# Two of the four sums of weight blocks of the gate/up units go from VectorE to GpSimd

## The chip, the core and the metric

The kernel runs on one core of a Trainium2 chip. The metric is the device time of one execution in microseconds (us). The core has five engines with queues of their own: TensorE (PE), VectorE (DVE), ScalarE (ACT), GpSimd (POOL) and SyncE (SP), which here only issues DMAs. Everything is computed in float32.

## The reference

Two layers (DEPTH = 2) of a streaming encoder run over 512 tokens of a new stream and 8 × 16 tokens of running streams, 640 tokens in all, with a model width of 1024:

```python
def _swiglu(h, w_gu, w_down):
    gu = h @ w_gu
    g, u = jnp.split(gu, 2, axis=-1)
    return (jax.nn.silu(g) * u) @ w_down
...
for l in range(DEPTH):
    xp = xp + 0.5 * _swiglu(_rmsnorm(xp, norm_ffn1[l]), w_ffn1_gu[l], w_ffn1_down[l])
    ...   # the mixer: one projection w_in, a short convolution, banded attention, gates, w_o
    xp = xp + mp
    xp = xp + 0.5 * _swiglu(_rmsnorm(xp, norm_ffn2[l]), w_ffn2_gu[l], w_ffn2_down[l])
```

The same is done for `xs`, the running streams. The feed-forward width D_FF is 2816, which is 22 tiles of 128. A final RMSNorm follows. The four feed-forward blocks are called a0, b0, a1 and b1 in the kernel; a mixer lies between a and b of each layer.

## The kernel before

All 640 tokens stay in SBUF, with the model width on the partitions (`x[0]` to `x[7]`, 128 x 640 each). Weights are streamed from HBM in chunks of 128 x 1024, in the order in which they are used, into three buffers `raw`. Each float32 factor is split into a high part (`hi`, a cast to fp32r on ScalarE) and a low part (`lo`, the rest, a subtraction on VectorE), and a product is three matmuls: hi·hi, hi·lo and lo·hi. For weights the parts are `whi` (L296) and `wlo` (L301), with three buffers each.

Most products of the feed-forward blocks are made "by seven". A product is cut into 2 x 2 blocks (two halves of the output or of the tokens, two halves of the depth), and seven block products do the work of eight, in return for sums of blocks of the weights and of the tokens. For a gate/up unit `j` (`gate_up`) the blocks are the up and the gate columns of one tile of D_FF and the even and odd tiles of the model width; for a unit of the down projection (`down_rows`, "rows" units, two for each group of four `j`, named r0 and r1) they are pairs of output rows and pairs of `j`. Both kinds take their weights as a unit of kind "gu": two chunks `ra` and `rb` from HBM, and four slabs for TensorE. `source(i)` makes the slabs. Slab 0 is `ra` as it came. For slab 1, two sums are put into a tile of their own, `s65`: `rb`'s two halves added, and that plus `ra`'s first half. For slab 2, two sums are put into `ra` in place: its first half plus `rb`'s first half, and `s65`'s first half plus its second half. Slab 3 is `rb`'s second half. The sums of slab 2 can only be made when slab 0 has been split, since they overwrite it. In the profile the four sums are `s<-raw`, `s<-s,raw`, `raw<-raw,raw` and `raw<-s,raw`, all of line L240 (`add`). There are 114 such units, 84 gate/up and 30 rows units. The mixer's units (kind "mix") have three sums of other halves ahead of one of slab 2.

In a gate/up unit TensorE does the seven products in the order X11, X21, XN6, XT5, XT7, X22, XT4, on three PSUM tiles `pa`, `pb` and `pc` from a pool of four banks. `pa` is added to four times, and copied or added out in between, so that each eviction has to end before the next product starts on it: X11's copy is `c1` (L819), XN6's is `u2` (L832), then VectorE takes `g` after XT7 (L240) and after XT4 (L848). After that ScalarE applies Silu (L849). In a rows unit `A` (`da` in the profile) is used in the same way; VectorE adds parts into `x` (`take`, L980), and others are copied out by ScalarE and added to `x` by accumulating DMAs that GpSimd issues (`send`, L975).

The order of instructions on each engine is set in two ways. In the parts between, a scheduler orders them by priority and by its own estimates of their durations; `manual_schedule` takes engines out of its hands. At a block's start and end TensorE, VectorE and ScalarE follow the program; from the third unit by seven on only TensorE does, and VectorE, ScalarE and GpSimd are placed by the scheduler. `prep`, `ahead` and `begin` set at which point of the program a slab is made.

Of the kernel before, what the change touches and what calls it, by code (L numbers as in the profile page):

```python
# [13 lines left out]
ALU = mybir.AluOpType  # L14
# [160 lines left out]
def trunk(ctx: ExitStack, tc: tile.TileContext, xin, wst, small, pbias, samplebias, kcache, vcache,  # L175
          yout, ko, vo, co):
    nc = tc.nc
    PE, DVE, ACT, POOL, SP = nc.tensor, nc.vector, nc.scalar, nc.gpsimd, nc.sync
# [40 lines left out]
    slabs, n = [], 0  # L219
# [9 lines left out]
    sums, pool, spool = {}, [None], [None]  # L229

    def load(i):
        while len(raws) <= i:
            n = len(raws)
            raw = wp.tile([P, CH], F32, tag="raw", name=f"raw{n}", bufs=3)
            raws.append(raw)
            SP.dma_start(raw, wst[n])
        return raws[i]

    def add(out, a, b):
        DVE.tensor_tensor(out=out, in0=a, in1=b, op=ALU.add)  # L240

    h1, h2 = slice(0, CH // 2), slice(CH // 2, CH)
# [3 lines left out]
    def source(i):  # L246

        if i >= len(slabs):
            return None
        if i not in sources:  # L250
            kind, n, arg = slabs[i]
            ra = load(n)
            if kind == "plain":
                sources[i] = [(ra, slice(0, arg))]
            elif arg == 0:
                sources[i] = [(ra, whole)]
            else:
                rb = load(n + 1)
                if arg == 1 and kind == "gu":
                    st = sums[n] = pool[0].tile([P, CH], F32, tag="s65", name=f"s65_{n}", bufs=1)  # L260
                    add(st[:, h2], rb[:, h1], rb[:, h2])
                    add(st[:, h1], st[:, h2], ra[:, h1])
                    sources[i] = [(st, whole)]
                elif arg == 1:

                    flush()
                    st = sums[n] = spool[0].tile([P, CH // 2], F32, tag="s6", name=f"s6_{n}", bufs=1)
                    add(ra[:, h1], ra[:, h1], rb[:, h1])
                    add(st, ra[:, h1], rb[:, h2])
                    add(rb[:, h1], rb[:, h1], rb[:, h2])  # L270
                    sources[i] = [(st, h1), (rb, h1)]
                elif arg == 2:
                    if kind == "gu":
                        add(ra[:, h1], ra[:, h1], rb[:, h1])
                    add(ra[:, h2], sums.pop(n)[:, h1], ra[:, h2])
                    sources[i] = [(ra, whole)]
                else:
                    sources[i] = [(rb, h2)]
        return sources[i]
# [3 lines left out]
    def prep(i):  # L283

        if i < len(ready) or i >= len(slabs):
            return
        assert i == len(ready)
        parts = source(i)
        hi = wp.tile([P, CH], F32R, tag="whi", name=f"whi{i}", bufs=3)
        lo = wp.tile([P, CH], F32R, tag="wlo", name=f"wlo{i}", bufs=3)  # L290
        ready.append((hi, lo))
        o = 0
        for src, c in parts:
            d = slice(o, o + c.stop - c.start)
            o = d.stop
            ACT.copy(hi[:, d], src[:, c])  # L296
            pending.append((lo[:, d], src[:, c], hi[:, d]))

    def flush():
        for lo, src, hi in pending:  # L300
            DVE.tensor_tensor(out=lo, in0=src, in1=hi.bitcast(F32), op=ALU.subtract)  # L301
        pending.clear()
# [16 lines left out]
    def ahead():  # L319

        source(len(ready))
# [157 lines left out]
    class Expand(Stats):  # L479
# [72 lines left out]
        def weights(self, m):  # L552


            if m == KT - 3:
                source(used[0] + 3)
            elif m == KT - 1:
                self.flush()
                ahead()
                flush()  # L560
                begin()
# [1327 lines left out]
```

## Time and profile before

| | |
|---|---|
| median of 3 runs | 2528.91 us (2527.09 to 2528.97) |
| profiled execution | 2527.76 us, its span 2526.0 us |
| busy: TensorE, VectorE | 2505.2 us, 2141.8 us |
| busy: ScalarE, GpSimd | 1286.6 us, 223.5 us |
| granted TensorE clock | 0.998 of full speed |

The span is from the first to the last instruction. Matmuls overlap: each one of 128 x 320 has some 0.31 us in the records, and the next one starts 0.15 us later, so a stall shows best as a start that comes later than that. VectorE's instructions overlap by some 0.08 us in the same way. A tile's last letter a or b in the profile names the block (a0 and a1, b0 and b1).

### The profile page before, as it was taken

To read this page: it belongs to the slowest core of one execution; us is meant where nothing else is said; L and a number is where in the kernel's file an instruction comes from. 1 tells how busy PE (TensorE), PEld (TensorE's weight loads), DVE (VectorE), ACT (ScalarE), POOL (GpSimd) and SP (SyncE) were. 2 spreads that over 40 slices of the span, in tenths; PEclk is the share of its full clock that TensorE was granted. 3 is DMA by queue.
4 is the path that set the end of the run, shared out by engine and by line. 5 is a ranking of instruction groups with operands and counts; after the bars stand their busy time and mean duration, and the time that the engine had idled before them with its cause. 6 is when DMAs were issued, how large, how long until landed. Compare 5 with 4: busy or idle time off the path is not lost.

```text
span 2526.0 us, 43134 instructions
## 1 busy us (share of the span) xinstructions
PE 2505.2 (99%) x17216; PEld 2443.9 (97%) x17216; DVE 2141.8 (85%) x3449; ACT 1286.6 (51%) x2038; POOL 223.5 (9%) x333
## 2 busy tenths in 40 slices
PE   8999999999999999999999999999999999999998
PEld 8999999888999999999999999998889999999998
DVE  7889999878677999998789999987786778898997
ACT  5445556665444545554455555556644445454553
POOL 0001112111000001110000111101110000011111
PEclk9999999999999999999999999999999999999999
DMA  3233445235222224443223444433342222243444
GB/s 136 76 95 104 120 118 134 107 109 166 76 83 85 76 101 115 107 108 100 84 84 96 119 115 115 106 103 124 130 137 84 76 84 77 91 108 108 117 110 104
DMA packets 99418, 264.51 MB, mean 105 GB/s; under 512 B 11056, under 2 KB 44976, under 8 KB 99216
## 3 DMA queue, kind: packets, MB, share of 16 engines
q1 hardware_dynamic: 69696, 221.80, 26.3%
q0 software_dynamic: 28800, 39.29, 8.7%
q8 instruction: 135, 2.21, 0.4%
q10 hardware_dynamic: 720, 0.65, 0.1%
q14 instruction: 67, 0.55, 0.1%
HBM read 223.75 MB, written 7.94 MB: 92 GB/s over the span
## 4 chain that ended last, share of the span: by engine, by line
PE 86%; DVE 7%; ACT 3%; DMA 2%; issue 2%; SPq 0%; ACTq 0%; DVEq 0%; POOLq 0%
PE pab L386 11%; PE paa L386 10%; PE pcb L386 6%; PE pca L386 5%; PE py L363 4%; PE daa L953 4%; PE po L363 4%; PE qa L386 4%; PE pdb L363 4%; PE dab L953 3%; PE pda L363 3%; PE pbb L386 3%; PE pba L386 2%; DVE wlo L301 2%; PE pv L1395 2%; PE ma_cv L386 2%
## 5 line engine op out<-in xcount | busy, mean ns | idle before, releaser
L296 ACT CAST whi<-raw 128x1024 fp32r<-128x1024 f32 (+1 forms) x566 | 508.1, 902 | 359.5 <-DVE raw L240 55.9
L301 DVE TENSOR_TENSOR wlo<-raw,whi 128x1024 fp32r<-128x1024 f32 (+1 forms) x566 | 583.4, 1034 | 126.2 <-ACT whi L296 121.2
L296 ACT CAST whi<-s 128x1024 fp32r<-128x1024 f32 (+1 forms) x150 | 142.2, 948 | 293.5 <-DVE s L240 156.5
L386 PE MATMUL pab<-xhib,whi 128*128 128x320 f32 x704 | 218.5, 310 | 1.0 <-DVE gb L240 0.6
L386 PE MATMUL pab<-xhib,wlo 128*128 128x320 f32 x704 | 217.2, 308 | 0.0
L386 PE MATMUL pab<-xlob,whi 128*128 128x320 f32 x704 | 217.2, 308 | 0.0
L386 PE MATMUL paa<-xhia,whi 128*128 128x320 f32 x640 | 198.1, 309 | 1.1 <-ACT c_a L766 0.5
L386 PE MATMUL paa<-xloa,whi 128*128 128x320 f32 x640 | 197.4, 308 | 0.0
L386 PE MATMUL paa<-xhia,wlo 128*128 128x320 f32 x640 | 197.4, 308 | 0.0
L301 DVE TENSOR_TENSOR wlo<-s,whi 128x1024 fp32r<-128x1024 f32 (+1 forms) x150 | 163.4, 1089 | 10.9 <-ACT whi L296 10.9
L975 POOL DMA_DIRECT2D x<-c_b x56 | 49.2, 1020 | 1084.9 <-DVE x L980 435.7
L386 PEld LDWEIGHTS pab<-xhib,whi 128*128 128x128 f32 x704 | 132.0, 188 | 2.5 <-DVE gb L240 1.2
L386 PEld LDWEIGHTS pab<-xlob,whi 128*128 128x128 f32 x704 | 132.1, 188 | 0.2
L386 PEld LDWEIGHTS pab<-xhib,wlo 128*128 128x128 f32 x704 | 132.0, 188 | 0.0
L975 POOL DMA_DIRECT2D x<-c_a x64 | 56.4, 1022 | 825.2 <-ACT whi L296 591.4
L386 PEld LDWEIGHTS paa<-xhia,whi 128*128 128x128 f32 x640 | 120.0, 188 | 1.9 <-ACT c_a L766 0.8
L240 DVE TENSOR_TENSOR s<-raw 128x512 f32<-128x512 f32 x114 | 78.2, 686 | 49.7 <-DMA raw<-in_wst 49.2
L386 PEld LDWEIGHTS paa<-xloa,whi 128*128 128x128 f32 x640 | 120.0, 188 | 0.1
L386 PEld LDWEIGHTS paa<-xhia,wlo 128*128 128x128 f32 x640 | 120.0, 188 | 0.0
L386 PE MATMUL pcb<-xhib,whi 128*128 128x320 f32 x352 | 108.6, 308 | 0.0
L386 PE MATMUL pcb<-xlob,whi 128*128 128x320 f32 x352 | 108.6, 308 | 0.0
L386 PE MATMUL pcb<-xhib,wlo 128*128 128x320 f32 x352 | 108.6, 308 | 0.0
(686 smaller groups left out, 7960.0 us busy)
## 6 DMA issues: line engine op xcount, KB each, us to landing
raw<-in_wst SPq DMA_DIRECT2D x380, 512.0 KB, 3.3
x<-c_a POOLq DMA_DIRECT2D x64, 160.0 KB, 3.7
x<-c_b POOLq DMA_DIRECT2D x56, 160.0 KB, 3.6
kc<-in_kcache SPq DMA_DIRECT2D x32, 256.0 KB, 3.8
vc<-in_vcache SPq DMA_DIRECT2D x16, 512.0 KB, 4.7
x<-u_a POOLq DMA_DIRECT2D x32, 160.0 KB, 4.2
x<-u_b POOLq DMA_DIRECT2D x28, 160.0 KB, 4.2
bias<-in_pbias POOLq DMA_DIRECT2D x16, 256.0 KB, 3.5
```

Of the source, the lines that this page charges most:

```text
L240: DVE.tensor_tensor(out=out, in0=a, in1=b, op=ALU.add)
L296: ACT.copy(hi[:, d], src[:, c])
L301: DVE.tensor_tensor(out=lo, in0=src, in1=hi.bitcast(F32), op=ALU.subtract)
L363: PE.matmul(ps[:, a, :HT], w, x[:, a * HT : (a + 1) * HT], start=first and j == 0, stop=last and j == 2)
L386: PE.matmul(ps, a, b, start=start and kp == 0 and j == 0, stop=stop and kp == NP - 1 and j == 2, skip_group_check=True)
L953: PE.matmul(ps[u], w, y, start=start and i == 0 and j == 0, stop=i == 1 and j == 2, skip_group_check=True)
L975: POOL.dma_start(x[ms[2 * u + r]][:, cols], z[:, u], accum_op=ALU.add)
L1395: PE.matmul(pv[t], xx[:, t * P : (t + 1) * P], w[:, kk * AW : (kk + 1) * AW], start=c == 0 and kk == 0 and j == 0, stop=c == KT // 2 - 1 a ...
```

## The change

The two sums of slab 2 of every "gu" unit are issued on GpSimd, as `tensor_tensor` instructions with the same operands in the same order. The two sums of slab 1 stay on VectorE, as do all sums of the mixer's units. Nothing else in the program text changes.

```diff
                 elif arg == 2:
                     if kind == "gu":
-                        add(ra[:, h1], ra[:, h1], rb[:, h1])
-                    add(ra[:, h2], sums.pop(n)[:, h1], ra[:, h2])
+                        POOL.tensor_tensor(out=ra[:, h1], in0=ra[:, h1], in1=rb[:, h1], op=ALU.add)
+                        POOL.tensor_tensor(out=ra[:, h2], in0=sums.pop(n)[:, h1], in1=ra[:, h2], op=ALU.add)
+                    else:
+                        add(ra[:, h2], sums.pop(n)[:, h1], ra[:, h2])
                     sources[i] = [(ra, whole)]
```

The two new instructions are lines L274 and L275 of the changed kernel, and all lines behind them move by two (L301 becomes L303, L980 becomes L982).

## The prediction

> **What bounds the kernel now.** I read the page first, then the table of stages, then the groups of VectorE, then the timeline of single units, and last what GpSimd does beside VectorE.
>
> ```profile
> span 2526.0 us, 43134 instructions
> PE 2505.2 (99%) x17216; PEld 2443.9 (97%) x17216; DVE 2141.8 (85%) x3449; ACT 1286.6 (51%) x2038; POOL 223.5 (9%) x333
> ```
>
> TensorE is busy for 99% of the span, and almost no idle time is there to be won. From the table of stages, a stretch inside a feed-forward block:
>
> ```profile
> core 0: us, PE busy (x) PEld busy (x) DVE busy (x) ACT busy (x) POOL busy (x), PEclk, DMA share, GB/s
> 300.00:400.00 100.00, 100.00 (x684) 100.00 (x683) 94.09 (x149) 52.23 (x77) 11.53 (x14) 1.00 0.40 110
> ```
>
> TensorE has no hole there, at full clock; VectorE is next with 94%, GpSimd is nearly free. So a change that only relieves VectorE is worth what few stalls of TensorE VectorE causes there; a change that makes a weight slab or an eviction late costs full price. The list of TensorE's waits (us in total, times, longest) gives those that VectorE causes in the units in question:
>
> ```profile
> PE pab L386 <- DVE gb L240: 0.6, 2, 0.5
> ...
> PE daa L953 <- DVE x L980: 0.6, 3, 0.2
> PE dab L953 <- DVE x L980: 0.6, 3, 0.2
> ...
> PE paa L386 <- DVE ga L240: 0.4, 1, 0.4
> ```
>
> **What is moved.** From the groups of VectorE by form:
>
> ```profile
> L240 DVE TENSOR_TENSOR raw<-s,raw 128x512 f32<-128x512 f32 x150 | 102.7, 684 | 0.0
> L240 DVE TENSOR_TENSOR raw<-raw,raw 128x512 f32<-128x512 f32 x150 | 102.3, 682 | 1.1 <-DMA raw<-in_wst 0.4
> L240 DVE TENSOR_TENSOR s<-s,raw 128x512 f32<-128x512 f32 x114 | 78.2, 686 | 1.9
> ```
>
> The third row counts the "gu" units: 114 (84 gate/up, 30 down rows). Each loses one add of the first two groups, 228 in all; the other 36 of each are the mixer's and stay. The built order of the changed program shows just that: 228 rows fewer on VectorE, 228 more on GpSimd, TensorE's and SyncE's order unchanged, 114 casts on ScalarE that now wait for GpSimd. One gate/up unit, VectorE, then ScalarE, then TensorE:
>
> ```profile
> 377.28 0.68 DVE L240 TENSOR_TENSOR s<-raw 128x512 f32<-128x512 f32 x1
> 377.88 1.22 DVE L301 TENSOR_TENSOR wlo<-raw,whi 128x1024 fp32r<-128x1024 f32 x1
> 379.02 0.48 DVE L240 TENSOR_TENSOR ga<-paa,c_a 128x320 f32<-128x320 f32 x1
> 379.42 0.68 DVE L240 TENSOR_TENSOR s<-s,raw 128x512 f32<-128x512 f32 x1
> 380.02 0.48 DVE L840 TENSOR_TENSOR ga<-ga,rhoa 128x320 f32<-128x320 f32 x1
> 380.42 0.48 DVE L240 TENSOR_TENSOR ua<-pca,c_a 128x320 f32<-128x320 f32 x1
> 380.82 0.68 DVE L240 TENSOR_TENSOR raw<-raw,raw 128x512 f32<-128x512 f32 x1
> 381.42 0.68 DVE L240 TENSOR_TENSOR raw<-s,raw 128x512 f32<-128x512 f32 x1
> 382.12 0.49 DVE L848 TENSOR_TENSOR ga<-paa,rhoa 128x320 f32<-128x320 f32 x1
> 382.52 1.22 DVE L301 TENSOR_TENSOR wlo<-s,whi 128x1024 fp32r<-128x1024 f32 x1
> ```
> ```profile
> 380.25 1.05 ACT L296 CAST whi<-s 128x1024 fp32r<-128x1024 f32 x1 [1.79 <-PE pca L386]
> 382.21 1.05 ACT L296 CAST whi<-raw 128x1024 fp32r<-128x1024 f32 x1 [0.91 <-DVE raw L240]
> 383.17 0.74 ACT L849 ACTIVATE ga<-ga 128x640 f32<-128x640 f32 x1
> 383.88 0.43 ACT L819 COPY c_a<-paa 128x320 f32<-128x320 f32 x1
> ```
> ```profile
> 383.68 0.31 PE L386 MATMUL pba<-xhia,whi 128*128 128x320 f32 x1
> 385.44 0.31 PE L386 MATMUL paa<-xhia,whi 128*128 128x320 f32 x1
> ```
>
> Removed: 382.12 − 380.82 = 1.30 us of VectorE a unit. None of it is on TensorE's path here: the second add ends at 382.10, the third slab is cast at 382.21, and TensorE goes on at 383.68 and 385.44 without a hole. A unit has seven products of 385.44 − 383.68 = 1.76 us, 12.3 us, so 8.1 units fall into 100 us and VectorE's load there drops from 94 to 83.5. That alone is worth nothing to TensorE.
>
> What waits behind the new adds: on ScalarE the cast of the third slab, behind it the Silu (L849) and the copy of the first product (L819), which frees `paa` for the matmul at 385.44. The copy ends at 384.31, so it has 1.1 us. On VectorE nothing waits for GpSimd by a semaphore but the third slab's `wlo`.
>
> **Price of an add on GpSimd.** The trace has no such add. The nearest rows are one-input copies of GpSimd, left alone and beside VectorE:
>
> ```profile
> L1370 POOL COPY ks<-k x8: 291/686/691, 473.9 to 1776.2; 128x128 f32<-128x128 f32 x8
> L1527 POOL COPY kc<-ks x32: 203/211/3011, 518.0 to 1853.1; 128x32 f32<-128x32 f32 x32
> ```
>
> Shortest 291 ns for 128 elements, 203 for 32: 0.92 ns an element on 0.17 us. For 512 elements that is 0.64 us if two inputs cost as one (lower bound), 1.11 us if they are read in turn. I take 1.1, because a second input has to come from somewhere; upper bound, with a wait in it, the 3.01 us of the longest copy. The Trainium skill, GPSIMD Engine Reference, section Performance versus the Vector engine, has 4497 ns for an add of 2048 elements, 1.96 times VectorE's; my estimate from it would be 1.34 us here, and by it the sum below would be some 20 us higher; no run so far shows it.
>
> Two adds in a row are then 2.2 us against 1.3. They may start earlier than before: the built order now has both sums of the second slab ahead of the first slab's `wlo` in 74 of 82 gate/up units I could match (37 of 81 before), so GpSimd starts when that `wlo` ends, at 379.10 in this unit instead of VectorE's 380.82, and would end at about 381.4, ahead of the old 382.10. Left alone, GpSimd is in time.
>
> **The port.** It is not left alone. What the 3.01 us copy was up against:
>
> ```profile
> 584.01 3.16 POOL L1527 COPY kc<-ks 128x32 f32<-128x32 f32 x2 [8.44 <-issue]
> ```
> ```profile
> 584.35 0.80 DVE L1178 TENSOR_TENSOR yc<-yc,b 128x640 f32<-128x640 f32 x1
> ...
> 586.42 0.67 DVE L301 TENSOR_TENSOR wlo<-s,whi 128x512 fp32r<-128x512 f32 x1
> 587.02 0.42 DVE L1537 CUSTOM_DVE_ANT_0 ss<-spss,sbias 128x272 f32<-128x272 f32 x1
> ```
>
> The second copy hangs through four VectorE instructions with both inputs in SBUF (the first and the last are shown), and ends 0.15 us after the first one that reads PSUM begins. In the other direction:
>
> ```profile
> 510.03 0.64 POOL L1365 COPY bd<-q 64x128 f32<-64x128 f32 x2 [1.87 <-DVE q L1362]
> ```
> ```profile
> 510.42 0.80 DVE L301 TENSOR_TENSOR wlo<-s,whi 128x512 fp32r<-128x512 f32 x1 [0.45 <-ACT whi L296]
> ```
>
> The same form took 0.67 us at 586.42, so this one lost 0.13 us, about the reading time of the 128-element copy beside it (128 × 0.92 ns). So reads of GpSimd and second inputs of VectorE exclude each other. The Trainium skill says so too: SBUF — State Buffer, section Who interferes with whom, calls it an exclusive lock for a whole instruction; the trace agrees, with 3.01 us against 0.21.
>
> Placed into the unit above, in its new order: GpSimd's first add 379.2 to 380.3, beside `ga<-paa` (PSUM, free) and against `ga<-ga,rho`, which slips from 379.5 to 380.3. Taking turns, that ends at 380.8 and the second add runs until 381.9, beside `ua<-pca`; `wlo<-s`, ready at 381.3 with its cast, slips to 381.9 and ends at 383.1. The built order now puts the eviction `ga<-paa,rho` (L848) behind it in 59 units (19 before): it ends at 383.6. The pool has four banks and a unit takes three, so the second product of the next unit, 383.68, writes that bank: nothing to spare. The free case costs 0. If GpSimd takes both turns, or an add has 1.3 us, the eviction ends at 383.9 to 384.3, 0.2 to 0.6 us late, with a restart of 0.1. Bounds 0 to 0.7 us a gate/up unit; I take 0.25, nearer the free case, for 84 units **21 us** (0 to 59). Below nothing it cannot go, as an added lock frees nobody.
>
> **Rows units.** Their second half (`r1`) shows what the new order costs, since a part of them has it already:
>
> ```profile
> 205.46 1.23 DVE L301 TENSOR_TENSOR wlo<-raw,whi 128x1024 fp32r<-128x1024 f32 x1 [0.45 <-ACT whi L296]
> 206.60 0.88 DVE L980 SCALAR_TENSOR_TENSOR x<-daa,x 128x320 f32<-128x320 f32 x2
> ```
> ```profile
> 207.04 0.31 PE L953 MATMUL dca<-ahia,wlo 128*128 128x320 f32 x1
> 207.54 0.42 PE L953 MATMUL daa<-t4hia,whi 128*128 128x320 f32 x1 [0.19 <-DVE x L980]
> 207.80 0.31 PE L953 MATMUL daa<-t4loa,whi 128*128 128x320 f32 x1
> ```
>
> With `wlo` ahead of the takes, starts that should lie 0.15 us apart (100 us for 684) lie 0.50 and 0.26 apart: 0.46 us. The waits above count six such units; the built order puts seven more `r1` units into this form: **3 us** (0 to 6). GpSimd's adds there lie beside four takes that read PSUM (1.7 us), so the port costs little. Its sends (`x<-c`, `x<-u`) that queue behind the adds wait up to 2 us more; the five `cap` buffers that they read come round again nearly two units, some 20 us, later: nothing, and a stall of `c` on ScalarE if that cover is gone.
>
> **Relief.** The three stalls of TensorE on `ga` and `gb` in the list above, 1.0 us idle and some 0.27 more each in the starts around them (0.46 lost for 0.19 idle in the case above), 1.8 us, may go with 1.3 us less work, and some of the six on `x`: **−3 us** (−6 to 0).
>
> Sum: 21 + 3 − 3 = +21 us. The profiled execution took 2527.76 us for its 2526.0 of span; the median is 1.15 above it. 2528.91 + 21 = **2550 us**.
>
> **Rivals.** *It fits* (0.2): turns are taken, an add has 1.1 us or less, the evictions just hold; 2530. For it: left alone the adds end earlier than now. Against: no spare at 383.68. *VectorE is shut out* (0.13): each add blocks it for a full 1.1 us and no PSUM reader covers it. Load 83.5 + 8.1 × 2.2 = 101 in 100 us where it has 94 and waits for the rest; some 7 us are lost in each of about twelve such stretches, +84: 2612. The 3.01 us copy speaks for it, the PSUM readers between against. *Faster* (0.05): if a pair of adds is through in under 2.2 us port included, VectorE's 1.3 us come ahead of every eviction, and the stalls it causes in these units go, six of 0.46 and three of 0.6: −5, with smaller ones below the list −6: 2523. Against: the new order makes more of that form. *That the change doesn't do what it says* has no chance, by the built order. The forecast itself, +5 to +70, has 0.62.
>
> About 0.2% (5 us) is what a measurement of this kernel can tell from no change. Slower by more: 0.62 + 0.13; within: 0.2; faster: 0.05. Range 2526 (all bounds at zero, a little relief) to 2600 (0.7 in every gate/up unit, with rows and part of the shut-out case).
>
> **What would show it.** Right: groups L274 and L275 on GpSimd, 114 each, mean over 1.1 us with a wide spread; `wlo` and `ga<-ga,rho` longer than 1.22 and 0.48 where they overlap; TensorE's waits for the takes of `x` (L982 there) doubled, and more and longer waits for `g` (DVE) and `c` (ACT); VectorE's busy share hardly lower. Wrong: adds of 0.7 us, unchanged `wlo` means, or a span below 2526; or waits of ScalarE for GpSimd of several us in each unit, which would be far above 2600.

## The result and the profile after

The changed kernel takes 2575.26 us (median of 4 runs, 2571.9 to 2577.26), the kernel before 2528.49 us beside it: ratio 1.0188, 95% interval 1.0176 to 1.02. That is +47 us, where +21 was forecast. The profiled execution took 2571.9 us. From its page, span and busy time, and the same stretch inside a feed-forward block as before:

```profile
span 2570.1 us, 43438 instructions
PE 2523.0 (98%) x17216; PEld 2445.0 (95%) x17216; DVE 2163.7 (84%) x3221; ACT 1289.1 (50%) x2038; POOL 554.3 (22%) x561
```
```profile
300.00:400.00 100.00, 96.63 (x649) 94.98 (x648) 91.55 (x125) 49.70 (x74) 31.86 (x28) 1.00 0.38 100
```

TensorE, which had no hole here, now has 3.4% of holes at the same full clock. Over the whole span VectorE has 228 instructions fewer and is busy for 22 us more. Who holds TensorE up (total us, times, longest):

```profile
PE paa L388 <- DVE ga L240: 9.6, 14, 1.5
PE pab L388 <- DVE gb L240: 6.7, 11, 1.3
...
PE daa L955 <- DVE x L982: 4.8, 13, 0.7
PE dab L955 <- DVE x L982: 4.0, 11, 0.7
PE paa L388 <- ACT c_a L834: 1.1, 5, 0.3
```

The take of `g` after XT7 made TensorE wait 3 times for 1.0 us before and 25 times for 16.3 us now; the takes of `x` in the rows units 6 times for 1.2 us and 24 times for 8.8 us. The take after XT4 (L850 now), where the prediction had put the loss, isn't in the list. The two sums on GpSimd (minimum/median/maximum in ns), and the groups of VectorE that grew:

```profile
L274 POOL TENSOR_TENSOR raw<-raw,raw x114: 1272/1290/1866, 67.4 to 2519.9; 128x512 f32<-128x512 f32 x114
```
```profile
L275 POOL TENSOR_TENSOR raw<-s,raw x114: 1280/1547/2296, 68.7 to 2521.1; 128x512 f32<-128x512 f32 x114
```
```profile
L303 DVE TENSOR_TENSOR wlo<-s,whi 128x1024 fp32r<-128x1024 f32 x114 | 214.7, 1884 | 9.6 <-ACT whi L298 7.8
...
L842 DVE TENSOR_TENSOR gb<-gb,rhob 128x320 f32<-128x320 f32 x42 | 45.9, 1093 | 1.3
L858 DVE TENSOR_TENSOR gb<-gb,rhob 128x640 f32<-128x640 f32 x44 | 44.6, 1013 | 0.8 <-ACT gb L851 0.8
L842 DVE TENSOR_TENSOR ga<-ga,rhoa 128x320 f32<-128x320 f32 x38 | 43.4, 1142 | 1.2
L858 DVE TENSOR_TENSOR ga<-ga,rhoa 128x640 f32<-128x640 f32 x40 | 38.0, 950 | 0.8 <-ACT ga L851 0.8
...
L982 DVE SCALAR_TENSOR_TENSOR x<-daa,x 128x320 f32<-128x320 f32 x64 | 28.1, 480 | 0.0
```

An undisturbed sum takes GpSimd 1.28 us against 0.68 on VectorE. `wlo<-s` went from 1215 to 1884 ns, `g*rho` from 485 to over 1090 (128x320) and from 817 to 950 and 1013 (128x640), all with both inputs in SBUF; `x<-daa,x`, which reads PSUM, stays at 480 (483 before). How one meeting looks, while a rows unit runs on TensorE. A unit's slabs are made ahead of it, so GpSimd's sums are here those of the gate/up unit that comes next; a rows unit's own sums lie in the gate/up unit ahead of it:

```profile
286.11 1.29 POOL L275 TENSOR_TENSOR raw<-s,raw 128x512 f32<-128x512 f32 x1
286.40 2.07 DVE L303 TENSOR_TENSOR wlo<-s,whi 128x1024 fp32r<-128x1024 f32 x1
```

GpSimd's sum runs at its full speed to 287.40, and VectorE's subtraction, which began beside it at 286.40, ends 1.07 us after that, nearly its whole 1.22: it has stood still until the sum had ended. The Trainium skill, SBUF — State Buffer, section Who interferes with whom, says that a VectorE instruction with two SBUF inputs contends with a GpSimd instruction that reads SBUF, and calls the contention an exclusive lock; the trace agrees, and here the lock lasts for the whole instruction and not for single elements. And how a lost stretch comes about, in that next gate/up unit:

```profile
287.57 1.06 ACT L298 CAST whi<-raw 128x1024 fp32r<-128x1024 f32 x1
...
290.33 1.21 DVE L303 TENSOR_TENSOR wlo<-raw,whi 128x1024 fp32r<-128x1024 f32 x1
...
291.57 1.57 SPq L236 DMA_DIRECT2D raw<-in_wst  x2
...
296.67 0.69 DVE L240 TENSOR_TENSOR s<-raw 128x512 f32<-128x512 f32 x1 [4.13 <-DMA raw<-in_wst]
...
298.01 1.22 DVE L303 TENSOR_TENSOR wlo<-raw,whi 128x1024 fp32r<-128x1024 f32 x1
...
299.14 0.48 DVE L240 TENSOR_TENSOR ga<-paa,c_a 128x320 f32<-128x320 f32 x1
...
299.68 0.41 PE L388 MATMUL paa<-xhia,whi 128*128 128x320 f32 x1 [1.52 <-DVE ga L240]
```

VectorE stands idle for 4.13 us because the second block of the unit after this one has not landed, and behind that stand, in the order that the scheduler gave it, both sums of that unit's slab 1, its slab 0's `wlo` and only then the take `ga<-paa,c_a` for which TensorE waits. The block was asked for at 291.57, when VectorE's `wlo` of this unit's slab 2 (290.33) had freed the raw buffer. Slab 2 itself was not what was late: its cast had ended at 288.63, and VectorE came to the `wlo` only 1.7 us later, from other instructions without a pause, since the stretched subtraction above stood in its queue.

### The profile page after: what moved, and what is told of

Same layout as the page of the kernel before. It is cut to its first block, busy times and chain, and to the rows that moved or that the text cites. A ratio compares the mean times of both kernels' runs of the same rounds, so it can differ in the third digit from the quotient of the medians.

```text
span 2570.1 us, 43438 instructions
## 1 busy us (share of the span) xinstructions
PE 2523.0 (98%) x17216; PEld 2445.0 (95%) x17216; DVE 2163.7 (84%) x3221; ACT 1289.1 (50%) x2038; POOL 554.3 (22%) x561
## 5 line engine op out<-in xcount | busy, mean ns | idle before, releaser
L298 ACT CAST whi<-raw 128x1024 fp32r<-128x1024 f32 (+1 forms) x566 | 508.1, 901 | 372.7 <-POOL raw L275 119.4
L303 DVE TENSOR_TENSOR wlo<-raw,whi 128x1024 fp32r<-128x1024 f32 (+1 forms) x566 | 583.1, 1033 | 107.1 <-ACT whi L298 104.5
L274 POOL TENSOR_TENSOR raw<-raw,raw 128x512 f32<-128x512 f32 x114 | 150.8, 1323 | 1463.6 <-DVE wlo L303 1280.8
L303 DVE TENSOR_TENSOR wlo<-s,whi 128x1024 fp32r<-128x1024 f32 (+1 forms) x150 | 239.6, 1597 | 17.4 <-ACT whi L298 15.6
L275 POOL TENSOR_TENSOR raw<-s,raw 128x512 f32<-128x512 f32 x114 | 184.9, 1622 | 0.0
```

What stands on the lines that cost most here:

```text
L274: POOL.tensor_tensor(out=ra[:, h1], in0=ra[:, h1], in1=rb[:, h1], op=ALU.add)
L275: POOL.tensor_tensor(out=ra[:, h2], in0=sums.pop(n)[:, h1], in1=ra[:, h2], op=ALU.add)
```

## The experiments

There are three theories: ORDER (VectorE's new order alone), PORT, later called DIRECT (VectorE's instructions stretched by GpSimd's reads), and LATE SLAB (slab 2, and with it the buffer and the next block, is late because GpSimd is slower). In the expectations QUEUE is DIRECT with what stands behind the stretched instructions, and LOOP is the way by the late block. Ratios are to the kernel before in the same runs, with 95% intervals.

**The sums left out, or turned into short fills.** In `e2_fill` `POOL.memset(ra[:, h1], 1.0)` and the same with `h2` stand in their place.

```diff
-                        POOL.tensor_tensor(out=ra[:, h1], in0=ra[:, h1], in1=rb[:, h1], op=ALU.add)
-                        POOL.tensor_tensor(out=ra[:, h2], in0=sums.pop(n)[:, h1], in1=ra[:, h2], op=ALU.add)
+                        sums.pop(n)
```

> The changed kernel without the two sums of slab 2: they are left out on both engines, and slab 2 is cast as it was loaded. VectorE's and ScalarE's order stays that of the changed kernel. Three theories for the +47 us. ORDER (VectorE now runs both sums of slab 1 and slab 0's wlo ahead of the take of XT7, whatever GpSimd does): stays near 2570 us, 25 late takes of XT7 as in the changed kernel. PORT (GpSimd's and VectorE's two-input instructions stretch each other): 2525 us or a few less, since VectorE has 156 us less to do and nothing is stretched; wlo 128x1024 back at 1.22 us. LATE SLAB (GpSimd's sums end later than VectorE's did, so slab 2's raw buffer comes free later and the next block lands later): also about 2525 us, sums of slab 1 wait for the DMA no more than the 33 times of before.

> GpSimd's two sums of slab 2 become two fills of the same halves (a constant is written, nothing is read, so slab 2's sums are left out). The same number of GpSimd instructions stands at the same place with the same waits of ScalarE behind them, and VectorE's order is that of the changed kernel. ORDER: about 2570 us. PORT: about 2525 us, wlo 128x1024 at 1.22 us, if a fill disturbs no read. LATE SLAB: between 2530 and 2570 us, the nearer to the upper end the closer a fill is to the 1.29 to 1.55 us of a sum.

Measured: 2529.2 us for both, ratios 1.0006 (0.9997 to 1.0015) and 1.0009 (1.0 to 1.0019). ORDER falls: in the changed kernel's very VectorE order nothing is lost. A slab 2 that is late by the 1.06 us of two fills costs nothing either. And there is nothing to be won: with the 228 sums gone from every engine the time is that of before. The page of `e1_no_adds`, and the place that lost 1.5 us above:

```profile
PE 2506.6 (99%) x17216; PEld 2443.8 (97%) x17216; DVE 2034.7 (81%) x3221; ACT 1292.1 (51%) x2038; POOL 223.5 (9%) x333
```
```profile
290.18 0.69 DVE L240 TENSOR_TENSOR s<-raw 128x512 f32<-128x512 f32 x1 [2.72 <-DMA raw<-in_wst]
...
291.51 1.22 DVE L302 TENSOR_TENSOR wlo<-raw,whi 128x1024 fp32r<-128x1024 f32 x1
292.64 0.48 DVE L240 TENSOR_TENSOR ga<-paa,c_a 128x320 f32<-128x320 f32 x1
```

Here too VectorE waits for the block, 2.72 us, with the take behind, and the take is just in time. So the new order is harmless by itself but has no slack left. Compared with this place, the changed kernel's `wlo` of slab 2 starts 0.75 us later behind its cast (2.76 us against 2.01), and its block takes 0.83 us longer from issue to the first sum on it (5.10 us against 4.27). GpSimd's sends, which there stand behind the sums, are under way beside the block for longer; that they make it slower was not tested. VectorE's busy time falls by 107 us here; in the changed kernel, with the same instructions, it is 2163.7 − 2034.7 = 129 us higher: that is what GpSimd's reads cost VectorE.

**Reads that nobody waits for.** `e8` adds two GpSimd sums a unit to the kernel before; `f5` adds two to `e1_no_adds`, `f6` one.

```diff
+                        for _ in range(2):   # e8, beside VectorE's own sums
+                            POOL.tensor_tensor(out=scr, in0=rb[:, :464], in1=rb[:, 512:976], op=ALU.add)
...
+                        for a in (ra[:, :464], ra[:, 512:976]):   # f5; f6 only the first
+                            POOL.tensor_tensor(out=scr, in0=s[:, :464], in1=a, op=ALU.add)
```

> The kernel before with its four sums on VectorE and its VectorE order unchanged, and beside them two GpSimd sums a unit that nobody waits for: they read the two halves of rb (464 of 512 columns each) and write a scratch tile of two bytes an element. Nothing of the computation is left out. ORDER: 2529 us, since the order is that of before. PORT: at least the 2575 us of the changed kernel, since VectorE has its 156 us still to do and is stretched as well; wlo 128x1024 near 1.9 us. LATE SLAB: 2529 to 2535 us, since no slab waits for GpSimd; wlo may stretch, but only a little of it reaches TensorE.

> GpSimd makes two sums a unit that read s and ra (464 of 512 columns each) and write a scratch tile; slab 2 is cast as it was loaded, so no cast waits for GpSimd (slab 2's sums are left out). VectorE's order is that of the changed kernel. The sums may start about 1.2 us earlier than in the changed kernel, since they don't wait for slab 0's wlo. DIRECT: 2560 to 2580 us, VectorE's wlo, ga*rho and sums stretched by 100 us or more in all. LATE SLAB: 2529 us.

> One sum into scratch a unit that nobody waits for, where the run with two cost 40 us; slab 2's sums are left out. If each read costs the same: 2549 us. If the first is covered by VectorE's idle time, since VectorE has 156 us less to do: 2529 to 2535 us. If the first already uses up all the slack: 2555 us or more.

Measured: `e8` 2682.67 us, 1.0618 (1.0602 to 1.0634), +155 us; `f5` 2568.82 us, 1.0161 (1.0146 to 1.0176), +40 us; `f6` 2548.61 us, 1.0085 (1.007 to 1.01), +21 us. So reads cost time with no slab waiting for them, and one sum a unit costs half of what two cost. In `e8`, where VectorE still has its own sums to do, two cost four times as much as in `f5`; but they read other tiles there, and the granted clock was 0.993 to 0.995, so the factor is not that of VectorE's load alone. Groups of `e8`, then waits of `f5`:

```profile
L240 DVE TENSOR_TENSOR s<-s,raw 128x512 f32<-128x512 f32 x114 | 143.2, 1256 | 1.9
```
```profile
PE daa L957 <- DVE x L984: 9.2, 7, 1.6
PE pab L390 <- DVE gb L240: 8.0, 13, 1.0
PE paa L390 <- DVE ga L240: 7.7, 12, 1.1
PE dab L957 <- DVE x L984: 6.6, 6, 1.6
```

`s<-s,raw` has 686 ns in the kernel before. In `f5` TensorE waits for the same two kinds of takes as in the changed kernel. The sums start earlier there than in the changed kernel and stretch other subtractions (`wlo<-raw` 1337 ns against 1218, `wlo<-s` only 1392), so its +40 is not a share of the +47.

**Slab 2 made late without reads.** Each sum becomes several fills: three and three (`f1`), two and two (`g_two`), one and two (`g_three`).

```diff
+                        for _ in range(3):
+                            POOL.memset(ra[:, h1], 1.0)
+                        for _ in range(3):
+                            POOL.memset(ra[:, h2], 1.0)
```

> Each of GpSimd's two sums of slab 2 becomes three fills (0.53 us each in the run with one fill), so GpSimd holds slab 2 back for about 3.2 us a unit, a little over the 2.9 us of the two sums in the changed kernel, and reads nothing. Slab 2's sums are left out. Since the runs before took ORDER away, two ways are left in which the reads cost the time. DIRECT (VectorE's own instructions beside GpSimd's reads are stretched, and what stands behind them in VectorE's queue is late): 2529 us, with ScalarE waiting for the fills as long as it waited for the sums (about 119 us in all). LATE SLAB (slab 2 is ready later, its raw buffer comes free later, the next block lands later): 2565 to 2580 us.

> Two fills in place of each of GpSimd's sums. A series of three fills came out at 0.67 us a fill, 4.0 us a unit, which is 1.1 us more than the 2.9 us of the changed kernel's two sums; two fills each come to 2.6 us, which is what two undisturbed sums would take (2 x 1.28 us). Nothing is read; slab 2's sums are left out; VectorE's order is that of the changed kernel. If slab 2 being late is what costs the time in the changed kernel too: 2550 us or more. If it costs only past a point that 2.6 us doesn't reach, and the changed kernel's loss is the stretching by its reads: 2529 to 2533 us.

> One fill in place of GpSimd's first sum and two in place of its second: slab 2 is 1.9 to 2.0 us late a unit, with no reads, in the changed kernel's VectorE order; slab 2's sums are left out. Two fills a unit (1.06 us) cost nothing and four (2.8 us) cost 37 us. PROPORTIONAL past 1.06 us: 2548 us. THRESHOLD (slack of some 2 us between slab 0's wlo and the cast of slab 2): 2529 to 2535 us.

Measured: 2575.15 us, 1.0186 (1.0171 to 1.0202); 2564.21 us, 1.0146 (1.0131 to 1.0161); 2550.18 us, 1.0094 (1.0079 to 1.0109). No VectorE group is longer than before by more than 10 ns. By the times alone LATE SLAB could make all of the loss too. But the slabs are not late by the same amount. The timeline of GpSimd while a rows unit runs, `g_two_fills` first and the changed kernel below:

```profile
283.16 0.53 POOL L275 MEMSET raw<- 128x512 f32 x1 [3.33 <-DVE wlo L306]
283.62 0.53 POOL L278 MEMSET raw<- 128x512 f32 x1
284.10 1.75 POOL L980 DMA_DIRECT2D x<-c_a  x2
285.17 2.48 POOL L980 DMA_DIRECT2D x<-u_a  x2
286.24 1.95 POOL L275 MEMSET raw<- 128x512 f32 x1
286.70 1.95 POOL L278 MEMSET raw<- 128x512 f32 x1
```
```profile
284.86 1.28 POOL L274 TENSOR_TENSOR raw<-raw,raw 128x512 f32<-128x512 f32 x1 [2.85 <-DVE wlo L303]
286.11 1.29 POOL L275 TENSOR_TENSOR raw<-s,raw 128x512 f32<-128x512 f32 x1
287.34 1.77 POOL L977 DMA_DIRECT2D x<-c_a  x2
288.46 2.46 POOL L977 DMA_DIRECT2D x<-u_a  x2
```

The scheduler had put the sends between the fills: slab 2 of the gate/up unit behind a rows unit is ready 5.5 us after GpSimd began on it in `g_two_fills`, and 2.5 us in the changed kernel. These three runs show that lateness of that size costs time, not that the changed kernel's does.

**The same with GpSimd's instructions of a unit kept together**, in fills and in sums: `order({mybir.EngineType.PE})` becomes `order({mybir.EngineType.PE, mybir.EngineType.Pool})`.

> GpSimd's order is kept as the program writes it, so that the instructions for slab 2 of a unit stay together and its DMA issues come before or after them. Three fills stand for each sum (0.47 us each in a row, 2.8 us a unit, as long as the two sums of the changed kernel); slab 2's sums are left out. VectorE's order is the changed kernel's in 31 of 87 stretches. DIRECT (the stretching makes the loss; slab 2 is in time, as the prediction had it): 2529 to 2537 us. LATE SLAB: 2560 us or more, as in the runs with fills whose rows units were 5 to 6 us late.

> The changed kernel with GpSimd's order kept as the program writes it, and nothing else: the yardstick for the run with fills. VectorE's order is that of the changed kernel throughout. 2575 us, if the place of the DMA issues doesn't matter; 2580 us or more if the copies that wait for them hold up ScalarE.

Measured: 2548.44 us, 1.0084 (1.0069 to 1.0099), and 2659.79 us, 1.0519 (1.0501 to 1.0536). The first lies between its two values, the second far above 2575 us. While a rows unit runs, the hand order has the sends ahead of the fills or sums, which makes slab 2 of the gate/up unit behind it some 7 to 8 us late in both runs (from the end of slab 0's `wlo`; 2.7 us in the changed kernel). TensorE's waits with fills, then with sums:

```profile
PE daa L957 <- ACT c_a L971: 7.8, 7, 2.5
PE dab L957 <- ACT c_b L971: 5.8, 7, 1.7
```
```profile
PE paa L388 <- ACT c_a L821: 33.7, 16, 2.8
PE pab L388 <- ACT c_b L821: 31.7, 16, 2.8
```

With fills there are 14 long waits in rows units for copies of ScalarE, in whose queue the cast of slab 2 waits for GpSimd, and next to none for the take after XT7, although slab 2 is 2.8 us or more late in gate/up units as well. With sums the loss is six times as large, but that does not speak for DIRECT: `y_hand_sums` has the changed kernel's order on VectorE and ScalarE, and most of what it loses beyond the changed kernel are the waits shown, 65.4 us (1.4 us there) for X11's copy, which stands behind the cast of the late slab. In the run with fills the scheduler ordered both engines otherwise. So the pair shows what LATE SLAB costs when the slab is 7 us late, and settles nothing for the changed kernel. Nor are the longer sums (1973 ns mean for the second) the reads' work alone: behind sends a fill, which reads nothing, took 1.95 us too.

**Parts of the change.** One sum, or one kind of unit, on GpSimd.

```diff
-                        POOL.tensor_tensor(out=ra[:, h2], in0=sums.pop(n)[:, h1], in1=ra[:, h2], op=ALU.add)
+                        add(ra[:, h2], sums.pop(n)[:, h1], ra[:, h2])   # e4
...
+                        on = POOL if n not in ro else DVE   # f3; f4 the other way round; ro: rows units
```

> Only the first of the two sums (ra's first half plus rb's) is on GpSimd, the second is back on VectorE. ORDER: VectorE gets one sum back and with it half of the old order; between 2535 and 2560 us. PORT: half of the GpSimd time, about half of the stretching: 2550 us, wlo 128x1024 near 1.5 us. LATE SLAB: VectorE's second sum now waits in VectorE's queue for GpSimd's first, which holds up everything behind it: 2575 us or more, with waits of VectorE for GpSimd that the changed kernel did not have.

> GpSimd's two sums in the 84 gate/up units alone; the 30 rows units (r0, r1) have theirs on VectorE as before. By the TensorE waits of the changed kernel's trace (late takes of XT7 in gate/up units about 27 us, late takes of x in rows units about 16 us) 2557 us. By the terms of the prediction (21 of 24 us in gate/up units) the rows units are worth only 3 us: 2570 us.

> GpSimd's two sums in the 30 rows units alone. By the TensorE waits of the changed kernel's trace 2544 us; by the terms of the prediction 2532 us. If the two halves (this run and the one with gate/up units alone) add up to more or less than the 47 us, the units hold each other up: r0 and r1 stand between gate/up units, and what is late in one of them is late in the next.

Measured: `e4` 2555.56 us, 1.0111 (1.0096 to 1.0126), +28, where VectorE's own second sum of slab 2 is what is stretched (1145 ns mean of the group, 684 before) and no wait of VectorE for GpSimd shows; `f3` 2567.37 us, 1.0153 (1.0136 to 1.017), +39; `f4` 2558.9 us, 1.0122 (1.0107 to 1.0137), +30. The kinds add up to 69 and not to 47. Waits of `f4`:

```profile
PE daa L958 <- DVE x L985: 6.7, 14, 1.3
PE dab L958 <- DVE x L985: 6.3, 12, 1.1
...
PE daa L958 <- ACT c_a L972: 5.2, 7, 0.9
PE dab L958 <- ACT c_b L972: 4.3, 6, 0.9
```

The second pair is not in the changed kernel: with sums on VectorE in the gate/up units the scheduler orders the rows units otherwise. So each half is a kernel of its own.

**Four raw buffers**, so that a block need not wait for slab 2 of the unit before.

```diff
-            raw = wp.tile([P, CH], F32, tag="raw", name=f"raw{n}", bufs=3)
+            if n in rbs:
+                raw = pool[0].tile([P, CH], F32, tag="rawb", name=f"raw{n}", bufs=2)
+            else:
+                raw = wp.tile([P, CH], F32, tag="raw", name=f"raw{n}", bufs=2)
```

> The changed kernel with four raw buffers where it had three, for the units by seven (rb gets two of its own, ra and the plain blocks keep two; five staging buffers become four, to make room). The second block of a unit then doesn't wait for slab 2 of the unit before. LOOP (VectorE's lag frees the raw buffer late, the block lands late, and VectorE stands idle up to 4.1 us on it with the take of XT7 behind): 2530 to 2540 us, and waits of VectorE for the block nearly gone. QUEUE (the take stands behind stretched instructions, the block's lateness is only a symptom): 2560 us or more. The scheduler moves the sums of slab 1 forward as well.

> The same four raw buffers in the kernel before, as the yardstick for the run with the changed kernel: 2520 to 2535 us, since its TensorE waits come to only 8.7 us. If the smaller ring for the plain blocks costs something, it is seen here.

Measured: 2568.59 us, 1.0163 (1.0146 to 1.018), and 2537.11 us, 1.0038 (1.0025 to 1.0051). The group of the first sum of slab 1, whose last column is VectorE's idle time before it, in the changed kernel and with four buffers:

```profile
L240 DVE TENSOR_TENSOR s<-raw 128x512 f32<-128x512 f32 x114 | 78.4, 688 | 83.2 <-DMA raw<-in_wst 82.8
```
```profile
L244 DVE TENSOR_TENSOR s<-raw 128x512 f32<-128x512 f32 x114 | 77.2, 677 | 0.0
```

The wait for the block is gone, and with it the waits for the take after XT7 from TensorE's list; but against its own yardstick +31 of the +47 us remain. The late block is a part of the way, not the whole cause. VectorE's order moved here too, so the 16 us are not a clean price of the block.

**Other places for the same work.** VectorE in the program's order, which has the take ahead of the sums (`order({PE, DVE})` for `order({PE})`); and the first sum into `rb`, so that it starts earlier:

```diff
-                        POOL.tensor_tensor(out=ra[:, h1], in0=ra[:, h1], in1=rb[:, h1], op=ALU.add)
+                        POOL.tensor_tensor(out=rb[:, h1], in0=ra[:, h1], in1=rb[:, h1], op=ALU.add)
```

> The changed kernel with VectorE's order in the gate/up and rows units after the first two of each block kept as the program writes it, so that the take of XT7 stands ahead of slab 0's wlo and of the two sums of slab 1 (which the scheduler had put ahead of it). GpSimd's sums stay. LOOP: the late block no longer holds the take, so the 20 us of late XT7 takes go; 2530 to 2555 us, unless the hand order makes new waits elsewhere. QUEUE: 2560 us or more, since the stretched instructions stand in the queue as before.

> The kernel before with VectorE's order kept as the program writes it in the same units as in the run h_after_take_first, so the take of XT7 is first and the sums are on VectorE. If the hand order itself makes ScalarE's copies late: 2700 us, as there. If it was the cast of slab 2, which waits for GpSimd with the copies behind it in ScalarE's queue: 2530 to 2560 us.

> The changed kernel with GpSimd's first sum written over rb's first half instead of ra's, so that it waits for VectorE's first sum of slab 1 and no longer for slab 0's wlo; slab 2 is then cast in two halves, one from rb and one from ra. Nothing of the computation is left out. The reads stay as many, and slab 2 is ready up to 1.3 us earlier. If the lateness adds to the stretching: 2560 us or less. If the stretching alone takes up the time: 2570 us or more, with the casts in halves on top.

Measured: 2716.46 us, 1.0749 (1.0733 to 1.0765); 2582.92 us, 1.0221 (1.0204 to 1.0238); 2595.7 us, 1.0271 (1.0256 to 1.0286). The program's order costs 56 us by itself, so it is no cure; with GpSimd's sums it is 134 us more, most of it in waits for ScalarE's copies, at a granted clock of 0.985:

```profile
PE pab L388 <- ACT c_b L821: 34.5, 31, 1.8
PE daa L955 <- ACT c_a L969: 33.0, 16, 2.4
```

The earlier sum is slower than the changed kernel by 20 us. Its mean is 1844 ns, about the longest of the changed kernel (1866): it now meets slab 0's `wlo`, which stands right ahead of the take after XT7 (`wlo<-raw` of 128x1024 has 1468 ns mean, 1220 in the kernel before). The 114 more casts and as many more subtractions, which slab 2 in two halves needs, are in the 20 us as well. No run of the 18 is faster than the kernel before.

**Read from the traces: where the 43 us go.** `e1_no_adds` and the changed kernel have the same instructions in the same order on TensorE, VectorE and ScalarE, so the starts of TensorE's matmuls can be compared one by one. Of the 43 us between the two spans, 23 are lost at the start of XT4 in the gate/up units, which needs the take after XT7; 9 at XN6 and XT7, most of it behind ScalarE's copies; and 7 at the last product of the rows units. For each of the 25 long waits for the take after XT7, VectorE came to the `wlo` that freed the raw buffer without a pause, and the cast of it had ended at least 0.2 us before: there VectorE's queue was late, and not slab 2. In 16 of the 25 VectorE had also stood idle for the block just before; in the other nine it had not. These nine places lose 7.3 us in the changed kernel, 10.0 in `f5_scratch`, which has reads and no slab that waits for them, and nothing in `g_two_fills`, which has no reads and a slab 2 that is 2.0 us late (2.9 in the changed kernel). Where it is as late as that, in `f1_long_fills`, they lose 1.5, in a slightly different order of VectorE. At the other 16 places the first three lose 14.2, 6.8 and 4.9 us. In the rows units 13 of the 24 waits for `x` are short and in `e1_no_adds` too (2.4 us there). The 11 long ones, 6.3 us, are new and all in r0 units, as here, with the second sum of that unit's slab 2:

```profile
248.04 1.56 POOL L275 TENSOR_TENSOR raw<-s,raw 128x512 f32<-128x512 f32 x1
...
248.77 1.92 DVE L303 TENSOR_TENSOR wlo<-s,whi 128x1024 fp32r<-128x1024 f32 x1
...
260.47 0.41 PE L955 MATMUL daa<-t4hia,whi 128*128 128x320 f32 x1 [0.65 <-DVE x L982]
```

From the stretched subtraction to the take VectorE has no pause, so what it lost ahead of the rows unit comes out in it.

## Why the prediction was right in sign and wrong in size

**Held.** The sign, the range (2526 to 2600), and each sign that was to show it: both groups of sums over 1.1 us with a spread, longer `wlo` and `ga*rho`, VectorE no less busy, more waits for `x` and `g`, some for `c`. That reads of GpSimd and two-input instructions of VectorE exclude each other was right, and `f5` and `e8` show that they cost time by themselves.

**The port term: 21 us, wrong place and too small.** It was laid at the take after XT4, behind `wlo<-s`, as 0.25 us for each of 84 units. Gate/up units alone cost 39 us, 0.46 a unit, inside its bounds of 0 to 0.7. TensorE never waited there; it waited for the next unit's take after XT7, most of a unit later (25 long waits, 16.3 us idle; with the short ones XT4 starts 23 us later in all). The step that failed is to follow the delay to the next eviction and stop. `wlo<-s` grew by 76 us (0.67 a unit) and `g*rho` by 51 and 14 (0.77 a gate/up unit). That lag stays in VectorE's queue. It frees the raw buffer later, and in 16 of the 25 waits it meets the wait for the block that the new order had put ahead of the take; in the other nine the queue alone makes the take late. The prediction counted the order of slab 0's `wlo` and of the sums, but only to tell when GpSimd could start, not to ask what stood behind the sums.

**The rows term: 3 us, against 30 for rows units alone.** What it counted came true: seven more waits of `x`, 13 in `e1_no_adds` for 6 before, at 0.2 us each. What failed is that it counted nothing else. It excused the port, since GpSimd's sums lay beside four takes that read PSUM. The takes are indeed untouched (480 ns), but those sums are the next gate/up unit's, and the second meets `wlo<-s` (2.07 us at 286.40). The rows units' own sums lie in the gate/up unit ahead, beside `g*rho` and `wlo<-s` (1.92 us at 248.77), and the delay stays in VectorE's queue until the rows unit's take: 11 new long waits in the changed kernel. It is the same step that failed, and this term was missed by the largest factor. The 30 us were measured with another order of VectorE, so they are not its share of the +47.

**Relief: −3 us.** In `e1_no_adds` the waits for the take after XT7 did go (0.2 us left of 1.0), while those for `x` doubled (2.4 us from 1.2). All 228 sums away give +1.4 us, with an interval around zero: near the 0 that this term and the rows term make together.

**The price.** 1.1 us was taken for a sum; alone it is 1.28. The Trainium skill, GPSIMD Engine Reference, section Performance versus the Vector engine, gave the estimate of 1.34, nearer, and the sum by it (some 20 us higher) would have been 2570: nearer too, but by the same step that failed. The cheaper price came from one-input copies, with a second read added to them. How much of the missing 26 us hangs on it no run tells.

**"Left alone, GpSimd is in time."** Not refuted, not shown. Lateness of 1.06 us costs nothing (`e2_fill`). With 2.8 us in gate/up units TensorE hardly waits for takes (`y_hand_fills`), but with another VectorE order. In the changed kernel ScalarE waits for the second sum 75 times, 119.4 us in all, but it is busy for only half of the span, and ahead of none of the 25 long waits for the take after XT7 did VectorE stand idle for slab 2's cast.

**The rivals.** *It fits* is out. *VectorE is shut out* had the mechanism of one meeting right, VectorE standing still until the sum ends, and the total too high (2612): the groups named above grew by 1.4 us a gate/up unit, not by the 2.2 us of both sums; `e8`, where VectorE keeps its sums as well, comes out beyond it, at +155 us.

**Open.** How the +47 divides in full. At nine places and at the 11 long waits in r0 units the traces show VectorE's stretched queue and nothing else; at the 16 with a late block the queue came first, but how much a block that takes longer to land adds, and why it does, was not tested. Reads alone (+40), late slabs alone in fills (+23 to +47, with slabs later than in the changed kernel), gate/up alone (+39) and rows alone (+30) each come near the whole, and don't add up. That they draw on one slack, VectorE's queue between two takes, fits all of them, but was not measured. A late slab of just the changed kernel's size in its very orders on GpSimd and VectorE was not tried, since the scheduler moved the instructions each time. In the three slowest runs the granted clock was lower too (0.993 to 0.995 in `e8`, 0.989 to 0.991 in `y_hand_sums`, 0.984 to 0.985 in `h_after`; 0.997 or more in all others); what of their time is due to that was not separated.

## What to carry to other kernels

Before work is moved off a busy engine, run the kernel with that work left out: here it would have shown that nothing was to be won, before any price of GpSimd mattered. Where a two-input sum of GpSimd met a subtraction of VectorE with both inputs in SBUF, in the two places shown, VectorE stood still until the sum had ended (2.07 and 1.92 us in place of 1.22), so look for places beside PSUM readers. Ask what queues behind each meeting, past the next eviction and up to the next pause of that engine, and whose work it is that lies there: with weights made ahead, the instructions beside a unit are often the next one's. And when instructions leave an engine that a scheduler orders, read what it now puts ahead of each eviction: the order may cost nothing by itself and still have lost the slack that covered a delay.

## What the runs showed that was not expected

The 228 sums on GpSimd for which nobody waits made the kernel before 155 us slower (`e8`), 0.68 us each, as much as a sum takes on VectorE itself; no run shows whether that is more than a coincidence. DMA issues on GpSimd are as long as sums (two sends in 1.75 us, two more in 2.48), so where a scheduler puts them between two steps of one slab decides how late it is; keeping GpSimd's instructions in program order made the changed kernel 85 us slower. Fills on GpSimd of 128x512, which read nothing, left every VectorE group at its old duration (`wlo<-s` at 1224 ns in `g_two_fills`).
